# Recurrence gates of a hybrid encoder block: block pairs in the two row halves of the array, sigmoids by halves of the partitions, no Square

## The chip, the cores and the metric

The kernel runs on one core of a Trainium2 chip. TensorE (PE in the profile) does matmuls, VectorE (DVE) and ScalarE (ACT) work element by element, GpSimd (POOL) issues some transfers, and SyncE (SP) issues most of them. The metric is the device time of one execution in microseconds; less is better. Of several runs the median counts.

## The reference

One layer: half an FFN step, a mixing step with two branches, half an FFN step again, on x of 512 tokens by 1024 features, all in float32. The part that matters here is branch A, a recurrence that runs forward and backward over the tokens:

```python
def _rglru_scan(xc, w_gates, b_gates, lam):
    xb = xc.reshape(B_, S, LRU_BLOCKS, LRU_BLOCK)          # 16 blocks of 64 features
    gates = jnp.einsum('bsni,gnio->gbsno', xb, w_gates).reshape(2, B_, S, W)
    gates = gates + b_gates[:, None, None, :]
    r = sigmoid(gates[0]); i = sigmoid(gates[1])
    log_a = -LRU_C * r * softplus(-lam)                    # LRU_C = 8
    a = exp(log_a)
    bx = sqrt(-expm1(2.0 * log_a)) * (i * xc)
    h = scan of h[t] = a[t] * h[t-1] + bx[t]

xr, gr, q, k, v, ga, gb = split(rmsnorm(x) @ w_in)
xc = depthwise conv of width 4 over the tokens of xr
A = (h_forward + h_backward) * gelu(gr)
B = neighbourhood attention of q, k, v (q and k RMS-normed per head)
x = x + (sigmoid(ga) * A + sigmoid(gb) * B) @ w_out
```

Each of the 16 blocks has its own 64 by 64 weight for r and for i, and that for each of the two directions.

## The kernel before

Features lie on the partitions, 128 at a time, and tokens along the free dimension, 512 of them. A tile of 128 features thus holds two blocks of the recurrence. Float32 accuracy comes from splitting each operand in a high part H (float32r, made by ACT) and the rest L (made by DVE), and from three matmuls: `mm3` is H·H, H·L and L·H. `load_w` loads a weight by SP's queue and splits it; its splits have high priority, so they stand early in ACT's and DVE's order.

The mixing step first makes `xr` (eight tiles f, 24 matmuls each, in `acc` banks of PSUM), and `conv` after each. Then `tok_group` makes q, k and v for each half of the heads: 96 matmuls in four banks `acc`, with four weight loads. `qk_raw` has ACT empty the banks of q and k (copy, then Square and a sum on DVE for the norm); `v_get` has DVE empty those of v. PSUM has four banks `acc` and four `aux`.

The recurrence `lru` is a generator, run for f 0 to 3 and then for f 4 to 7 (here: the first half and the second half). `weave` calls it between the chunks of the other products, `RATE` steps at a time; `heads`, the attention, is a second such lane. For each f it makes gates for both directions d: the gate matmuls into `aux` banks, sigmoids on ACT, i times xc on DVE (tile `ix`), a tanh on ACT (tile `th`). When all eight (f, d) have that, it goes over them with exp, then roots, then the scans on DVE. With th = tanh(x), x = −log a, the kernel gets 1 − a² as (1 + a²)·th; Square makes a². So each activation table is loaded once in a half and not for every tile.

In `heads`, `rq` is one over the norm of q and k (`nc.scalar` Sqrt, then a reciprocal on DVE); eight multiplies scale the raw q and k tiles (`qk`); `start` transposes them and splits them into `qh`, `ql`, `kh`, `kl`; `scores` multiplies, with 64 rows a head, two heads side by side.

Instructions are written in this order, and the framework's scheduler sets the final order of each engine from priorities and its own estimates. `after(i, prev)` orders two instructions. An engine runs its own list in order; a wait on one holds all behind it.

Of the kernel before, what the change touches and what calls it, by code (L numbers as in the profile page):

```python
# [9 lines left out]
F32 = mybir.dt.float32  # L10
F32R = mybir.dt.float32r
AF = mybir.ActivationFunctionType
ALU = mybir.AluOpType
# [54 lines left out]
def block_kernel(ctx: ExitStack, tc, a, out):  # L68
# [27 lines left out]
    def aux_t():  # L96
        return aux.tile([P, T], F32, tag="aux", name=nm("aux"))
# [34 lines left out]
    def load_w(src, n, act=True):  # L132
        raw = raw_t()
        H, L = hl_t()
        s = slice(0, n)
        ld = nc.sync.dma_start(raw[:, s], src[:, s])
        if nld[0] < 8:
            tc.keep_in_program_order(ld)
        nld[0] += 1
        with tc.high_priority():  # L140
            split(raw[:, s], H[:, s], L[:, s], act)
        return H, L
# [53 lines left out]
        nc.scalar.activation(r, ps, AF.Copy)  # L196
        return r, rcol, vx

    def after(i, prev):

        i, prev = getattr(i, "ins", i), getattr(prev, "ins", prev)
        tc.add_manual_dep(i, prev.name, mybir.DependencyInfo(
            mybir.DependencyClass.NoSync, mybir.DependencyReason.DATA), reason="order")


    mark = {}
# [338 lines left out]
    sp = const.tile([P, 16], F32, name="sp")  # L545
    nc.vector.tensor_scalar(sp, nlam, 0.0, None, ALU.max)
    nc.vector.scalar_tensor_tensor(sp, pol, 2.0, sp, ALU.mult, ALU.add)
    sp8 = const.tile([P, 16], F32, name="sp8")
    nc.vector.tensor_scalar(sp8, sp, 8.0, None, ALU.mult)
    sn8 = const.tile([P, 16], F32, name="sn8")  # L550
    nc.vector.tensor_scalar(sn8, sp, -8.0, None, ALU.mult)
    gq8 = const.tile([P, 1], F32, name="gq8")
# [27 lines left out]


    last_act = [None]

    def lru(fs):
        un = []
        cuts = {}

        def cut(f):
            if f in fs:
                cuts[f] = big_t(F32R, n="ch"), big_t(F32R, n="cl")  # L590
                split(xc[f], *cuts[f])

        cut(fs[0])
        for f in fs:
            gH, gL = load_w(a["wgate"][f], T)
            cut(f + 1)
            cH, cL = cuts.pop(f)
            yield
            for d in range(2):
                rt = []  # L600
                for g in range(2):
                    q = d * 2 + g
                    s = slice(q * P, (q + 1) * P)
                    ps = aux_t()
                    mm3(ps, gH[:, s], gL[:, s], cH, cL, True, True)
                    t = big_t(n="gate")
                    i = nc.scalar.activation(t, ps, AF.Sigmoid, bias=small[:, C_BG + f * 4 + q : C_BG + f * 4 + q + 1])
                    if last_act[0] is not None:
                        after(i, last_act[0])
                    rt.append(t)  # L610
                r, ix = rt
                nc.vector.tensor_tensor(ix, ix, xc[f], ALU.mult)
                th = big_t(n="th")
                tanh = nc.scalar.activation(th, r, AF.Tanh, scale=sp8[:, f * 2 + d : f * 2 + d + 1])
                un.append((f, d, r, ix, th))
                yield
        for f, d, r, ix, th in un:
            exp = nc.scalar.activation(r, r, AF.Exp, scale=sn8[:, f * 2 + d : f * 2 + d + 1])
            after(exp, tanh)
            sq = big_t(n="a2")  # L620
            nc.scalar.activation(sq, r, AF.Square)
            nc.vector.scalar_tensor_tensor(th, sq, 1.0, th, ALU.add, ALU.mult)
            yield
        for f, d, av, ix, th in un:
            last_act[0] = nc.scalar.activation(th, th, AF.Sqrt)
            after(last_act[0], exp)
            nc.vector.tensor_tensor(ix, ix, th, ALU.mult)
            yield
        h = None
        for f, d, av, ix, th in un:  # L630
            if d == 0:
                h = th
                nc.vector.tensor_tensor_scan(h, av, ix, 0.0, ALU.mult, ALU.add)
            else:
                nc.vector.tensor_tensor_scan(th[:, ::-1], av[:, ::-1], ix[:, ::-1], 0.0, ALU.mult, ALU.add)
                nc.vector.tensor_tensor(h, h, th, ALU.add)
                A[f] = h
            yield
# [263 lines left out]
def layouts(inp):  # L902

    f = lambda n: np.asarray(inp[n])
    con = np.ascontiguousarray
    o = {}
    x = f("x")[0].reshape(ROWS, NCB, QC, KT, P)
    o["x"] = con(x.transpose(3, 4, 1, 0, 2)).reshape(KT, P, T)

    def feat(w):  # L910
        k, n = w.shape
        return con(w.reshape(k // P, P, n // P, P).transpose(2, 1, 0, 3)).reshape(n // P, P, k)

    for i in (1, 2):
        w = f(f"w_ffn{i}_gu")[0]
        g, u = feat(w[:, :DFF]), feat(w[:, DFF:])
        n = NPLAIN[i - 1]
        o[f"w{i}gu"] = con(np.stack([g, u], 1)[:n]).reshape(2 * n, P, D)

        b = np.stack([g, u], 0)[:, n:].reshape(2, (FT - n) // 2, 2, P, 2, D // 2)  # L920
        o[f"w{i}s"] = con(b.transpose(1, 4, 0, 3, 2, 5)).reshape((FT - n) // 2, 4, P, D)
        d = f(f"w_ffn{i}_down")[0].reshape(FT // 2, 2, P, 2, T)
        o[f"w{i}d"] = con(d.transpose(3, 0, 2, 1, 4)).reshape(2, FT // 2, P, 2 * T)
    w = f("w_in")[0].reshape(D, 7, D)
    o["wxr"] = feat(w[:, 0])
    o["wg3"] = np.concatenate([feat(w[:, c]) for c in (1, 5, 6)], 0)
    qkv = w[:, 2:5].reshape(4, 2, P, 3, 2, T)
    o["wqkv"] = con(qkv.transpose(3, 4, 0, 2, 1, 5)).reshape(6, 4, P, 2 * T)
    o["wout"] = feat(f("w_out")[0])
    wg = f("lru_w_gates")[0]  # L930
    bd = np.zeros((KT, P, 4, P), wg.dtype)
    for b in range(16):
        s = slice((b % 2) * 64, (b % 2) * 64 + 64)
        bd[b // 2, s, :, s] = wg[:, :, b].reshape(4, 64, 64).transpose(1, 0, 2)
    o["wgate"] = bd.reshape(KT, P, 4 * P)
    col = lambda v: np.asarray(v).reshape(-1, KT, P).transpose(2, 1, 0).reshape(P, -1)
    o["small"] = con(np.concatenate([
        col(f("norm_ffn1")[0]), col(f("norm_mix")[0]), col(f("norm_ffn2")[0]),
        col(f("conv_w")[0]), col(f("conv_b")[0]),
        col(f("lru_b_gates")[0].reshape(4, D)), col(f("lru_lambda")[0]),  # L940
        np.tile(f("q_norm")[0], 2)[:, None], np.tile(f("k_norm")[0], 2)[:, None]], 1))


    rp = f("rel_pos_bias")[0]
    t = np.full((NH, ROWS, QC, 3, 2, ROWS, QC), -1.0e30, rp.dtype)
    for ty, n in enumerate((0, 1, 3)):
        for p in range(QC):
            c = n * QC + QC - 1 - p
            cs = min(max(c - 8, 0), GW - 16)
            for k in range(cs, cs + 16):  # L950
                hf, kc = divmod(k - KSTART[n], QC)
                for r in range(ROWS):

                    t[:, r, p, ty, hf, :, kc] = rp[:, r : r + ROWS, k - c + 15]
    o["rpb"] = t.reshape(NH, P, 6 * P)
    return o
# [18 lines left out]
```

## Time and profile before

| | |
|---|---|
| three runs, median (lowest, highest) | 1137.01 us (1136.99, 1138.92) |
| the profiled execution | 1136.66 us |
| its span from first to last instruction | 1134.9 us |
| granted TensorE clock | 1.0 |
| PE, DVE, ACT busy | 1126.8, 837.1, 617.3 us |
| first gate matmul, and first of the second half | 384.21, 453.10 us |
| first scores | 524.87 us |

The profile's rows give start and duration in us, engine, line of the code, operation, what is written and read, shape, and a count where equal neighbours are merged; in brackets how long the engine was idle before, and on what. Matmuls overlap: each shows about 0.39 us for 512 columns though they start much closer together, so the distance of starts is what counts.

### The profile page before, as it was taken

The numbers are of one execution on the slowest core, as the hardware profiler recorded it, in microseconds if no ns is written. First come the engines' busy times: TensorE is split into PE (matmuls) and PEld (weight loads), VectorE is DVE, ScalarE is ACT, GpSimd is POOL, SyncE is SP. The second block draws the span as 40 slices with busy tenths as digits, with TensorE's granted clock in tenths as the row PEclk, the third lists the DMA queues.
The fourth block names the chain that finished last, engine by engine and source line by source line (L and its number), as shares of the span: only waits on it lengthen the run. The fifth ranks groups of instructions, "written<-read, shape, count | busy, mean of one in ns | idle before, by whom it ended". The sixth has DMA issues, their size and how long they took to land.

```text
span 1134.9 us, 17275 instructions
## 1 busy us (share of the span) xinstructions
PE 1126.8 (99%) x6874; PEld 994.4 (88%) x6874; DVE 837.1 (74%) x1288; ACT 617.3 (54%) x924; POOL 19.3 (2%) x52
## 2 busy tenths in 40 slices
PE   9999999999999999999999999999999999999998
PEld 7899999988888888888788887778999999998886
DVE  7898888884836779788855577758688888894542
ACT  8554544563624696995564266756445545464330
POOL 0000000000000000010110000000000000000000
PEclk9999999999999999999999999999999999999999
DMA  8242333443333352353443232345123333253421
GB/s 274 81 131 80 122 97 109 132 133 103 121 102 104 98 169 68 124 165 93 137 143 103 93 102 90 107 167 186 56 80 124 95 108 116 89 171 94 130 75 38
DMA packets 43554, 130.70 MB, mean 115 GB/s; under 512 B 5968, under 2 KB 8272, under 8 KB 43472
## 3 DMA queue, kind: packets, MB, share of 16 engines
q1 hardware_dynamic: 39600, 119.36, 33.6%
q0 software_dynamic: 3296, 9.97, 2.9%
q8 instruction: 54, 0.88, 0.3%
q10 hardware_dynamic: 576, 0.26, 0.1%
q14 instruction: 28, 0.23, 0.1%
HBM read 121.17 MB, written 8.39 MB: 114 GB/s over the span
## 4 chain that ended last, share of the span: by engine, by line
PE 95%; DVE 3%; ACT 2%; issue 0%; DMA 0%; DVEq 0%; ACTq 0%
PE acc L260 29%; PE acc L146 11%; PE acc L145 11%; PE acc L147 10%; PE aux L260 5%; PE aux L145 4%; PE aux L146 4%; PE aux L147 4%; PE acc L668 3%; PE acc L667 3%; PE acc L669 3%; PE aux L796 1%; DVE wl L121 1%; PE aux L785 1%; DVE so L769 1%; ACT wh L118 1%
## 5 line engine op out<-in xcount | busy, mean ns | idle before, releaser
L118 ACT ACTIVATE wh<-wraw 128x1024 fp32r<-128x1024 f32 (+3 forms) x242 | 241.4, 1000 | 323.5 <-PE acc L260 98.5
L121 DVE TENSOR_TENSOR wl<-wraw,wh 128x1024 fp32r<-128x1024 f32 (+3 forms) x254 | 291.5, 1151 | 131.0 <-ACT wh L118 130.4
L260 PE MATMUL acc<-s,wh 128*128 128x256 f32 x1216 | 220.6, 283 | 0.0
L260 PEld LDWEIGHTS acc<-s,wh 128*128 128x128 f32 x1216 | 188.8, 190 | 0.0
L260 PE MATMUL acc<-s,wl 128*128 128x256 f32 x608 | 172.1, 283 | 0.0
L145 PE MATMUL acc<-xh,wh 128*128 128x512 f32 x304 | 120.4, 396 | 0.0
L146 PE MATMUL acc<-xl,wh 128*128 128x512 f32 x304 | 119.5, 393 | 0.0
L147 PE MATMUL acc<-xh,wl 128*128 128x512 f32 x304 | 118.9, 391 | 0.0
L260 PEld LDWEIGHTS acc<-s,wl 128*128 128x128 f32 x608 | 115.8, 190 | 0.0
L260 PE MATMUL acc<-xh,wl 128*128 128x256 f32 x304 | 86.1, 283 | 0.0
L260 PE MATMUL acc<-xl,wh 128*128 128x256 f32 x304 | 86.1, 283 | 0.0
L260 PE MATMUL acc<-xh,wh 128*128 128x256 f32 x304 | 86.0, 283 | 0.0
L667 PE MATMUL acc<-wh,xh 128*128 128x512 f32 x192 | 75.5, 393 | 0.0
L668 PE MATMUL acc<-wh,xl 128*128 128x512 f32 x192 | 74.8, 390 | 0.0
L669 PE MATMUL acc<-wl,xh 128*128 128x512 f32 x192 | 74.8, 389 | 0.0
L294 DVE TENSOR_TENSOR wraw<-wraw,pair 128x1024 f32<-128x1024 f32 x57 | 69.6, 1221 | 0.8
L145 PE MATMUL aux<-hh,wh 128*128 128x512 f32 x176 | 68.5, 389 | 0.0
L146 PE MATMUL aux<-hl,wh 128*128 128x512 f32 x176 | 68.5, 389 | 0.0
L147 PE MATMUL aux<-hh,wl 128*128 128x512 f32 x176 | 68.5, 389 | 0.0
L146 PE MATMUL acc<-hl,wh 128*128 128x512 f32 x176 | 68.5, 389 | 0.0
L145 PE MATMUL acc<-hh,wh 128*128 128x512 f32 x176 | 68.5, 389 | 0.0
L147 PE MATMUL acc<-hh,wl 128*128 128x512 f32 x176 | 68.5, 389 | 0.0
(195 smaller groups left out, 2221.5 us busy)
## 6 DMA issues: line engine op xcount, KB each, us to landing
wraw<-wqkv SPq DMA_DIRECT2D x24, 512.0 KB, 3.6
wraw<-wg SPq DMA_DIRECT2D x24, 512.0 KB, 3.5
wraw<-w1d SPq DMA_DIRECT2D x22, 512.0 KB, 3.6
wraw<-w2d SPq DMA_DIRECT2D x22, 512.0 KB, 3.6
pair<-w2s SPq DMA_DIRECT2D x20, 512.0 KB, 3.6
wraw<-w2s SPq DMA_DIRECT2D x20, 512.0 KB, 3.6
wraw<-w1s SPq DMA_DIRECT2D x18, 512.0 KB, 3.6
pair<-w1s SPq DMA_DIRECT2D x18, 512.0 KB, 3.6
```

The source lines that it names most:

```text
L118: nc.scalar.activation(H, raw, AF.Copy)
L121: nc.vector.tensor_tensor(L, raw, H.bitcast(F32), ALU.subtract)
L145: nc.tensor.matmul(ps, wh, xh, start=first, stop=False)
L146: nc.tensor.matmul(ps, wh, xl, start=False, stop=False)
L147: nc.tensor.matmul(ps, wl, xh, start=False, stop=last)
L260: nc.tensor.matmul(o, w_[:, c], x_, start=first and m + k == 0 and w_ is H and x_ is xh_, stop=m + k == 4 and w_ is L, skip_group_check=True)
L294: nc.vector.tensor_tensor(t, t, o, ALU.add)
L667: nc.tensor.matmul(pss[j], xh[kk][:, tj], H[:, s], start=kk == 0, stop=False)
L668: nc.tensor.matmul(pss[j], xl[kk][:, tj], H[:, s], start=False, stop=False)
L669: nc.tensor.matmul(pss[j], xh[kk][:, tj], L[:, s], start=False, stop=kk == KT - 1)
L769: nc.vector.tensor_tensor_reduce(so[:, cs], ps[hp][:, cs], bm[:, BTYPE[n]], -1.0, 3.0e38, ALU.add, ALU.min, nmx[:, i : i + 1])
L785: nc.tensor.transpose(pT[:, q * P : (q + 1) * P], pt[:, q * P : (q + 1) * P], ident)
```

## The change

The gate weights were laid out as 128 by 128 matrices with two 64 by 64 blocks on the diagonal and zeros beside them: for each f and d one such matrix for r and one for i. Now they are packed without the zeros: rows 0 to 63 hold the weights of the tile's first block, rows 64 to 127 those of its second, and the 128 columns are r and i side by side. For each f and d there are two banks `ps[b]`, one a block; three matmuls of 64 rows fill each, and those of the two blocks alternate, so that they stand in the two row halves of the array. A bank then has r in its partitions 0 to 63 and i in 64 to 127, so four sigmoids of 64 partitions put the parts in place where two of 128 did. The load of `wgate` is half as wide.

The first matmul of a group waits for the last sigmoid of the group two before it (`evicted`). The Square goes: with th = tanh(x/2) the root of th times (1 + a) is the root of 1 − a², so DVE multiplies `ix` by (1 + a) where it multiplied `th` by (1 + a²).

```diff
-                rt = []
-                for g in range(2):
-                    q = d * 2 + g
-                    s = slice(q * P, (q + 1) * P)
-                    ps = aux_t()
-                    mm3(ps, gH[:, s], gL[:, s], cH, cL, True, True)
-                    t = big_t(n="gate")
-                    i = nc.scalar.activation(t, ps, AF.Sigmoid, bias=small[:, C_BG + f * 4 + q : C_BG + f * 4 + q + 1])
-                    if last_act[0] is not None:
-                        after(i, last_act[0])
-                    rt.append(t)
-                r, ix = rt
+                c = slice(d * P, (d + 1) * P)
+                ps = [aux_t() for _ in range(2)]
+                mm = None
+                for W, X in ((gH, cH), (gH, cL), (gL, cH)):
+                    for b in (0, 1):
+                        o = slice(b * HD, (b + 1) * HD)
+                        prev, mm = mm, nc.tensor.matmul(
+                            ps[b], W[o, c], X[o], start=W is gH and X is cH, stop=W is gL)
+                        if prev is not None:
+                            after(mm, prev)
+                        elif len(evicted) > 1:
+                            after(mm, evicted[-2], True)
+                r, ix = (big_t(n="gate") for _ in range(2))
+                q = C_BG + f * 4 + d * 2
+                for b in range(2):
+                    for g, t in enumerate((r, ix)):
+                        o = slice(g * HD, (g + 1) * HD)
+                        i = nc.scalar.activation(t[b * HD : (b + 1) * HD], ps[b][o], AF.Sigmoid,
+                                                 bias=small[o, q + b : q + b + 1])
+                        if last_act[0] is not None:
+                            after(i, last_act[0])
+                evicted.append(i)
                 nc.vector.tensor_tensor(ix, ix, xc[f], ALU.mult)
                 th = big_t(n="th")
-                tanh = nc.scalar.activation(th, r, AF.Tanh, scale=sp8[:, f * 2 + d : f * 2 + d + 1])
+                tanh = nc.scalar.activation(th, r, AF.Tanh, scale=sp4[:, f * 2 + d : f * 2 + d + 1])
...
             exp = nc.scalar.activation(r, r, AF.Exp, scale=sn8[:, f * 2 + d : f * 2 + d + 1])
             after(exp, tanh)
-            sq = big_t(n="a2")
-            nc.scalar.activation(sq, r, AF.Square)
-            nc.vector.scalar_tensor_tensor(th, sq, 1.0, th, ALU.add, ALU.mult)
+            nc.vector.scalar_tensor_tensor(ix, r, 1.0, ix, ALU.add, ALU.mult)
...
-            gH, gL = load_w(a["wgate"][f], T)
+            gH, gL = load_w(a["wgate"][f], 2 * P)
```

The scheduler also moves other work. Three places follow; names are tiles with their numbers, and a word in brackets is the engine that is waited for.

PE, the last f of the second half. Before, four gates of three matmuls in a row:

```order
L145 MATMUL aux_4757<-ch_4657,wh_4722 128x512 [waits Activation_49]
L146 MATMUL aux_4757<-cl_4658,wh_4722 128x512 [waits DVE_49]
L147 MATMUL aux_4757<-ch_4657,wl_4723 128x512
L145 MATMUL aux_4763<-ch_4657,wh_4722 128x512 [waits Activation_49]
L146 MATMUL aux_4763<-cl_4658,wh_4722 128x512
L147 MATMUL aux_4763<-ch_4657,wl_4723 128x512
L145 MATMUL aux_4772<-ch_4657,wh_4722 128x512 [waits Activation_49]
L146 MATMUL aux_4772<-cl_4658,wh_4722 128x512
```

Now two groups of three pairs, here with one matmul of the value product between them:

```order
L609 MATMUL aux_4769<-ch_4665,wh_4734 128x512 [waits PE_49,Activation_49]
L609 MATMUL aux_4770<-ch_4665,wh_4734 128x512 [waits PE_49]
L609 MATMUL aux_4769<-cl_4666,wh_4734 128x512 [waits DVE_49]
L609 MATMUL aux_4770<-cl_4666,wh_4734 128x512
L609 MATMUL aux_4769<-ch_4665,wl_4735 128x512
L609 MATMUL aux_4770<-ch_4665,wl_4735 128x512
L679 MATMUL acc_4591<-wh_4806,xh_3102 128x512
L609 MATMUL aux_4786<-ch_4665,wh_4734 128x512 [waits PE_49,Activation_49]
L609 MATMUL aux_4787<-ch_4665,wh_4734 128x512 [waits PE_49]
```

As many matmuls as before, and each group's first one waits for ACT.

ACT, start of the second half. Before:

```order
L607 ACT_TABLE_LOAD
L607 ACTIVATE gate_4551<-aux_4547,small 128x512
L118 ACTIVATE wh_4662<-wraw_4661 128x1024
L607 ACTIVATE gate_4557<-aux_4553,small 128x512
L614 ACTIVATE th_4560<-gate_4551,sp_3675 128x512
L607 ACTIVATE gate_4566<-aux_4562,small 128x512
L607 ACTIVATE gate_4572<-aux_4568,small 128x512
L614 ACTIVATE th_4575<-gate_4566,sp_3675 128x512
L118 ACTIVATE ch_4583<-xc_4084 128x512
L718 ACT_TABLE_LOAD
L718 ACTIVATE rq_4932<-rq_4932 128x64
```

Now:

```order
L620 ACT_TABLE_LOAD
L620 ACTIVATE gate_4555<-aux_4547,small 64x512
L118 ACTIVATE wh_4670<-wraw_4669 128x1024
L620 ACTIVATE gate_4556<-aux_4547,small 64x512
L620 ACTIVATE gate_4555<-aux_4548,small 64x512
L620 ACTIVATE gate_4556<-aux_4548,small 64x512
L627 ACTIVATE th_4562<-gate_4555,sp_3675 128x512
L620 ACTIVATE gate_4572<-aux_4564,small 64x512
L620 ACTIVATE gate_4573<-aux_4564,small 64x512
L620 ACTIVATE gate_4572<-aux_4565,small 64x512
L118 ACTIVATE wh_4734<-wraw_4733 128x256
L620 ACTIVATE gate_4573<-aux_4565,small 64x512
```

The eight sigmoids stand where four stood, and the root for `rq` (L718) with its table load is no longer between the f's: it stands behind the last exp of the half.

DVE, the scale of the raw q and k tiles. Before, it stood among the gates of the second half (L612 is i times xc):

```order
L719 RECIPROCAL rq_4932<-rq_4932 128x64
L121 TENSOR_TENSOR wl_4723<-wraw_4721,wh_4722 128x512
L724 TENSOR_TENSOR qk_4351<-qk_4351,rq_4932 128x512
L724 TENSOR_TENSOR qk_4356<-qk_4356,rq_4932 128x512
L724 TENSOR_TENSOR qk_4361<-qk_4361,rq_4932 128x512
L724 TENSOR_TENSOR qk_4366<-qk_4366,rq_4932 128x512
L121 TENSOR_TENSOR wl_4729<-wraw_4727,wh_4728 128x1024
L612 TENSOR_TENSOR gate_4631<-gate_4631,xc_3989 128x512
```

Now it comes behind all of them and behind the multiplies by 1 + a (L634), mixed with those by the root (L639), ahead of the scans:

```order
L634 SCALAR_TENSOR_TENSOR gate_4778<-gate_4777,gate_4778 128x512
L634 SCALAR_TENSOR_TENSOR gate_4795<-gate_4794,gate_4795 128x512
L731 RECIPROCAL rq_4932<-rq_4932 128x64
L639 TENSOR_TENSOR gate_4556<-gate_4556,th_4562 128x512
L639 TENSOR_TENSOR gate_4573<-gate_4573,th_4579 128x512
L736 TENSOR_TENSOR qk_4351<-qk_4351,rq_4932 128x512
L736 TENSOR_TENSOR qk_4356<-qk_4356,rq_4932 128x512
L736 TENSOR_TENSOR qk_4361<-qk_4361,rq_4932 128x512
L121 TENSOR_TENSOR wl_5079<-wraw_5077,wh_5078 128x1024
L736 TENSOR_TENSOR qk_4366<-qk_4366,rq_4932 128x512
L639 TENSOR_TENSOR gate_4634<-gate_4634,th_4640 128x512
```

The reciprocal and the eight multiplies moved from the middle of the gates to the queue that ends in `kl`.

More of the change, by code (lines that the diff above doesn't have):

```diff
@@ L197, in rstd, with after @@
         return r, rcol, vx
-    def after(i, prev):
+    def after(i, prev, sync=False):
         i, prev = getattr(i, "ins", i), getattr(prev, "ins", prev)
         tc.add_manual_dep(i, prev.name, mybir.DependencyInfo(
-            mybir.DependencyClass.NoSync, mybir.DependencyReason.DATA), reason="order")
+            mybir.DependencyClass.Sync if sync else mybir.DependencyClass.NoSync, mybir.DependencyReason.DATA), reason="order")
     mark = {}
@@ L547, in block_kernel @@
     nc.vector.scalar_tensor_tensor(sp, pol, 2.0, sp, ALU.mult, ALU.add)
-    sp8 = const.tile([P, 16], F32, name="sp8")
-    nc.vector.tensor_scalar(sp8, sp, 8.0, None, ALU.mult)
+    sp4 = const.tile([P, 16], F32, name="sp4")
+    nc.vector.tensor_scalar(sp4, sp, 4.0, None, ALU.mult)
     sn8 = const.tile([P, 16], F32, name="sn8")
@@ L582, in block_kernel @@
     last_act = [None]
+    evicted = []
     def lru(fs):
@@ L930, in layouts @@
     wg = f("lru_w_gates")[0]
[L931 to L935, printed above, removed]
+    o["wgate"] = con(wg.reshape(2, 2, KT, 2, 64, 64).transpose(2, 3, 4, 0, 1, 5)).reshape(KT, P, 4 * 64)
     col = lambda v: np.asarray(v).reshape(-1, KT, P).transpose(2, 1, 0).reshape(P, -1)
+    bg = f("lru_b_gates")[0].reshape(2, 2, KT, 2, 64).transpose(1, 4, 2, 0, 3).reshape(P, 4 * KT)
     o["small"] = con(np.concatenate([
```

2 lines of the change are left out of this document (1 added, 1 removed).

## The prediction

> **What bounds the kernel now.** I read the page first, then the busy time by stretches, then the timelines of PE, ACT and DVE around the gates.
>
> ```profile
> PE 1126.8 (99%) x6874; PEld 994.4 (88%) x6874; DVE 837.1 (74%) x1288; ACT 617.3 (54%) x924; POOL 19.3 (2%) x52
> PE 95%; DVE 3%; ACT 2%; issue 0%; DMA 0%; DVEq 0%; ACTq 0%
> ```
>
> PE carries the chain that ended last almost alone, so a matmul taken out can shorten the run. The averages of ACT and DVE (54% and 74%) say little about the gates, which all stand between 384 and 525 us. That part in five stretches (first half of the gates; the query product; the key product; second half of the gates with the value product; from there to the first scores):
>
> ```profile
> core 0: us, PE busy (x) PEld busy (x) DVE busy (x) ACT busy (x) POOL busy (x), PEclk, DMA share, GB/s
> 384.00:409.60 25.60, 25.60 (x113) 20.68 (x112) 21.38 (x29) 24.38 (x38) 2.54 (x8) 1.00 0.61 192
> 409.60:431.30 21.70, 21.70 (x97) 18.00 (x96) 17.30 (x24) 21.64 (x34) 0.00 (x0) 1.00 0.29 87
> 431.30:453.10 21.80, 21.80 (x97) 18.02 (x97) 21.19 (x32) 10.97 (x19) 0.00 (x0) 1.00 0.25 76
> 453.10:485.70 32.60, 32.60 (x145) 26.98 (x144) 23.82 (x34) 30.14 (x45) 1.35 (x3) 1.00 0.41 129
> 485.70:524.80 39.10, 39.10 (x177) 32.19 (x175) 34.18 (x46) 26.50 (x42) 2.92 (x5) 1.00 0.46 129
> ```
>
> Here ACT is nearly as full as PE: 24.38 of 25.60, 21.64 of 21.70, and 30.14 of 32.60. The change gives PE less to do and ACT more, in just these stretches.
>
> **PE's part.** The same timeline shows a plain run and the one place where matmuls of 64 rows already stand in pairs, the scores (L759):
>
> ```profile
> 453.10 0.39 PE L145 MATMUL aux<-ch,wh 128*128 128x512 f32 x1
> ...
> 524.55 0.39 PE L669 MATMUL acc<-wl,xh 128*128 128x512 f32 x1
> 524.87 0.38 PE L759 MATMUL aux<-kh,qh 64*128 64x256 f32 x2
> 525.09 0.28 PE L759 MATMUL aux<-kl,qh 64*128 64x256 f32 x2
> 525.21 0.28 PE L759 MATMUL aux<-kh,ql 64*128 64x256 f32 x2
> ...
> 525.56 0.28 PE L759 MATMUL aux<-kh,ql 64*128 64x256 f32 x2
> 525.78 0.66 PE L733 MATMUL aux<-ident,qk 128*128 128x128 f32 x4
> ...
> 526.63 0.48 PE L667 MATMUL acc<-wh,xh 128*128 128x512 f32 x1
> 526.94 0.39 PE L668 MATMUL acc<-wh,xl 128*128 128x512 f32 x1
> ```
>
> Matmuls of 512 columns follow each other every 0.227 us (the key product's 96 fill the 21.80 us of its stretch). A pair of 256-column ones in the two row halves takes 0.12 (525.09 to 525.21), about half of that, so a pair costs what its columns cost once; I take 0.227 for a pair of 512 columns. Gates now: 96 matmuls, 21.8 us. Afterwards: 48 pairs, 10.9. Saved: 10.9 us of PE.
>
> Every stretch of pairs also pays to get in and out. Entry: 0.32 where 0.227 is usual, +0.09. First pair: 0.22 for 0.12, +0.10. Exit: 525.56 to 525.78, again 0.22 for 0.12, +0.10. The first full matmul behind: 0.31 for 0.227, +0.08 (read behind transposes, its nearest row). Together 0.37 a stretch; as bounds, 0.20 (entry and one more) and 0.5. The order of the changed kernel has 12 stretches: 7 in the first half, where matmuls of other products stand between the groups, 5 in the second. That is 4.4 us, and PE alone keeps 6.5.
>
> **ACT's part.** Rows of the second half, and of groups:
>
> ```profile
> 454.89 1.28 ACT L607 ACT_TABLE_LOAD   x1
> 456.19 0.69 ACT L607 ACTIVATE gate<-aux,small 128x512 f32<-128x512 f32 x1
> 456.77 1.05 ACT L118 ACTIVATE wh<-wraw 128x1024 fp32r<-128x1024 f32 x1
> 457.72 0.68 ACT L607 ACTIVATE gate<-aux,small 128x512 f32<-128x512 f32 x1
> 458.29 0.72 ACT L614 ACTIVATE th<-gate,sp 128x512 f32<-128x512 f32 x1
> 458.90 1.26 ACT L607 ACTIVATE gate<-aux,small 128x512 f32<-128x512 f32 x2
> ...
> 462.60 0.26 ACT L718 ACTIVATE rq<-rq 128x64 f32<-128x64 f32 x1
> ...
> 487.16 3.77 ACT L618 ACTIVATE gate<-gate,sn 128x512 f32<-128x512 f32 x6
> ```
>
> ```profile
> L621 ACT ACTIVATE a<-gate 128x512 f32<-128x512 f32 x16 | 8.9, 617 | 0.0
> ```
>
> From start to start a sigmoid takes 0.57, a split of 1024 columns 0.95, a tanh 0.61, an exp 0.62. A Square, 0.62 long, counts as 0.52, since the next starts 0.1 before its end, and a `ch` split of the same size too. No ACT row covers 64 partitions. Bounds for the half sigmoid: 0.57 (a full one) and 0.285 (half of it). I take 0.57, because a split of 1024 columns is 1.05 long and a Square of 512 is 0.62 on the same 128 partitions: time goes with the columns, and these stay 512. So 64 half sigmoids replace 32 whole ones, +18.2 us of ACT; the 16 Squares (L621) go, −8.3; the gate weight splits halve in width, some −1.6 (an estimate, 0.2 each).
>
> The second half is then no longer PE's. From its first sigmoid to its last tanh ACT has 32 half sigmoids (18.2), 8 tanh (4.9), 7 splits of 1024 (6.7), two ch splits (1.0) and one half-wide gate weight split (0.3, an estimate): 31.1 us. PE has 96 full matmuls (21.8), 24 pairs (5.4) and 5 stretches' switches (1.9): 29.1. Before, PE needed 32.6 there, and ACT was busy for 30.14. The Trainium skill's page TensorEngine Tiling (Performance Considerations, PSUM Bottleneck) warns of this, that tiling speeds up the matmuls and not the emptying of PSUM; by that rule alone the second half would end 2.0 us after PE's sum, which is near what the steps below give from rows.
>
> **Second half, step by step.** T is the time from its first gate matmul, 453.10 before. ACT's table load is tied to the end of the key product, T 1.8 (454.89), and ends at 3.1. Each group's first matmul waits for the last sigmoid of the group two before it; a sigmoid's result is there some 0.15 after the next one starts (it is 0.69 long, the next starts at 0.57). The fourth group is free at T 8.1 but its sigmoid ends at 9.5: PE waits 1.5. The eighth is free at 24.4 and starts at 25.9: another 1.5. Then the value eviction: in DVE's order the four `v` stand behind the last group's multiply, which waits for ACT at T 32.7; first `v` out at 34.3, where PE wanted its bank at 32.4: 1.9. PE's total to the scores is 71.75 (524.87) − 5.4 + 1.9 + 4.9 = 73.1.
>
> DVE is later still. The reordered row scale of the attention (L719, L724 before; `rq`, `qk`) moves from 462.9 to behind the last exp:
>
> ```profile
> 462.89 0.55 DVE L719 RECIPROCAL rq<-rq 128x64 f32<-128x64 f32 x1 [0.88 <-ACT rq L718]
> ...
> 464.02 2.49 DVE L724 TENSOR_TENSOR qk<-qk,rq 128x512 f32<-128x512 f32 x4
> ...
> 517.57 1.20 DVE L633 TENSOR_TENSOR_SCAN th<-gate,gate 128x512 f32<-128x512 f32 x1
> 518.68 1.20 DVE L121 TENSOR_TENSOR wl<-wraw,wh 128x1024 fp32r<-128x1024 f32 x1
> 519.80 0.69 DVE L636 TENSOR_TENSOR th<-th,th 128x512 f32<-128x512 f32 x1
> ...
> 523.80 0.74 DVE L742 SCALAR_TENSOR_TENSOR kl<-aux,small,kh 128x512 fp32r<-128x512 f32 x1
> ```
>
> ACT: from 3.1, the 31.1 above, a table 1.3, 8 exp 5.0, one split 0.95 = T 41.4; table and `rq` root: 43.1. Then on DVE in one queue up to `kl`: reciprocal 0.5, 8 multiplies `qk` and 8 `gate` at 0.6 = 9.6, 4 reductions 2.4, 8 scans at 1.11 = 8.9, 4 adds 2.4, 5 splits at 1.13 = 5.7, small ones 0.4, `ql` and `kl` 1.4: 31.3. With 0.6 of waits on splits whose buffers PE frees late, `kl` is ready at T 75.0. Before, its matmul started at 525.09, T 72.0. Second half: 3.0 us worse.
>
> **First half.** The same count: 24 pairs save 5.4; 7 switches cost 2.6; the waits for sigmoids, with ACT now 4 us fuller (16 × 0.57 − 8 × 0.52 − 0.8), come to 1.3 in six places of 0.1 to 0.4, the last where the key product takes over banks that ACT empties. Net 1.5 us earlier at the second half's start. DVE, 21.19 of 21.80 busy in the stretch before, would let it come at most 2.6 earlier: the second half's first `cl` stands at the end of its queue.
>
> **The rest.** Halved loads of `wgate` (SP's queue) save bytes that nothing waits for. From the first scores on the engines' orders are the same, but for a handful of rows; what is late there stays late to the end. New scales and operands (`sp4`, `ix` for `th`) keep count and shape: 0, covered by equal rows.
>
> **Sum.** −1.5 + 3.0 = +1.5 us on the profiled 1136.66. The median of the runs, 1137.01, is 0.35 above that execution; on it I forecast 1138.5. A measurement tells about 0.2%, 2.3 us, from no change: this is inside.
>
> **Rivals.** (a) Slower: the first half gives nothing back. Place: ACT between 384 and 431, where it had 1.3 us free of 47.3 and gets 4 more; its query evictions free the key product's banks. Price: the 1.5 are lost, 1137.0 + 3.0 = 1140.0. It decides when the gain at the second half's start falls under 0.8. For it: those two stretches; against: by my count only 0.4 reaches PE there, and ACT is half empty next (10.97 of 21.80).
>
> (b) Faster: ACT keeps up, as it would if half the partitions took half the time (the lower bound 0.285: ACT's sum then is 22.0 against 29.1). PE's 6.5 stand whole: 1130.5. Against it: columns, not partitions, set the rows above. The Trainium skill's page ScalarE: Activation LUTs (Step-by-step: what each stage is for) says one element per cycle and lane whatever the function; by it 64 partitions take as long as 128. No row here shows it.
>
> (c) The pairs don't run side by side at 512 columns. Then first half +3.9, second 73.1 + 5.4 − 71.75 = 6.8: 1147.7. L759 speaks against it.
>
> **Numbers.** Forecast, within 0.2%: 0.50. (a) with all that ends over 1139.3: 0.33; (b) with all under 1134.7: 0.15; (c) 0.02. So faster 0.15, same 0.50, slower 0.35. The likeliest case alone spans 1136.8 (a switch at 0.20 in the first half's seven places, −1.2, and a DVE queue free of waits, −0.5) to 1140.9 (a switch at 0.5, +0.9, and (a)'s 1.5). The range reaches to 1134.0 for part of (b) and to 1141.5.
>
> **What would show it.** Pairs of `ch` 0.23 apart, 64x512 sigmoids near 0.68 long; PE idle before the fourth and eighth group of the second half and before the first product after it, 1.5 to 2 each; scores waiting for DVE `kl`; the second half's first gate matmul near 451.6 and the first `kl` matmul near 526.6 (453.10 and 525.09 before). I am wrong if ACT is not in one piece from T 3 to 41, or half sigmoids are shorter, or `kl` comes before PE.

## The result, and the profile after

The changed kernel takes 1149.63 us (median of four runs; 1148.88 to 1152.53) where the kernel before takes 1137.0: ratio 1.0114, 95% interval 1.0102 to 1.0126, 12.6 us slower. The forecast was 1138.5, with a range up to 1141.5; the direction that it thought second likeliest came, and by more than its range allowed. The profiled execution of the changed kernel took 1149.65 us, its span is 1147.9 (before 1134.9).

The profile page's busy times, and the shares of the chain that ended last:

```profile
PE 1127.2 (98%) x6874; PEld 986.5 (86%) x6874; DVE 834.8 (73%) x1288; ACT 631.1 (55%) x938; POOL 19.2 (2%) x52
...
PE 86%; ACT 9%; DVE 3%; issue 1%; DMA 0%; ACTq 0%; DVEq 0%
```

PE lost 9 points of the chain and ACT took 7 of them. The five stretches, cut at the same places of the program as before (window, its length, then busy time and count of PE, PEld, DVE, ACT and POOL, PE's granted clock, DMA share, GB/s):

```profile
384.00:410.60 26.60, 23.63 (x113) 16.18 (x113) 17.27 (x23) 26.05 (x37) 2.55 (x8) 1.00 0.55 177
410.60:436.00 25.40, 24.64 (x113) 19.48 (x110) 16.89 (x24) 24.99 (x35) 0.00 (x0) 1.00 0.24 74
436.00:457.40 21.40, 19.38 (x86) 15.48 (x86) 21.40 (x29) 14.78 (x27) 0.00 (x0) 1.00 0.20 56
457.40:496.20 38.80, 34.01 (x144) 24.62 (x142) 20.08 (x33) 36.91 (x53) 0.00 (x0) 0.87 0.39 112
496.20:537.70 41.50, 39.61 (x179) 32.47 (x178) 40.40 (x57) 27.61 (x39) 4.27 (x7) 1.00 0.45 121
```

Before, PE was busy all through these 141 us. Now it stands idle 5.75 us in the first three stretches (26.60 − 23.63, 25.40 − 24.64, 21.40 − 19.38), 4.8 in the fourth and 1.9 in the fifth, and in the fourth its granted clock is 0.87. ACT is the full engine: 26.05 of 26.60, 24.99 of 25.40, 36.91 of 38.80. What PE waited for, in the same part (total, times, longest):

```profile
PE aux L609 <- ACT gate L620: 8.4, 7, 2.4
PE acc L679 <- ACT qk L692: 2.0, 1, 2.0
PE aux L771 <- DVE kl L754: 1.9, 1, 1.9
PE acc L679 <- DVE v L703: 0.3, 1, 0.3
```

Two rows by tile give the place in time (durations smallest/median/largest in ns, then first and last start in us, here from the second half on): the gate matmuls of the second half and the scores' `kl`.

```profile
L609 PE MATMUL aux<-ch,wh x16: 392/493/792, 457.2 to 487.0; 64*128 64x512 f32 x16
L771 PE MATMUL aux<-kl,qh x12: 277/280/383, 538.0 to 558.8; 64*128 64x256 f32 x12
```

The second half starts at 457.2 (before 453.1; forecast 451.6) and the scores at 538.0 (before 525.1; forecast 526.6). That is 12.9 of the 13.0 us: all is lost ahead of the first scores, 4.1 in the first half and 8.8 in the second.

Where ACT's time goes is seen in three rows of its timeline and two by line. A row "x4" is four instructions back to back:

```profile
472.80 0.73 ACT L627 ACTIVATE th<-gate,sp 128x512 f32<-128x512 f32 x1
473.53 2.80 ACT L620 ACTIVATE gate<-aux,small 64x512 f32<-64x512 f32 x4
476.36 1.06 ACT L118 ACTIVATE wh<-wraw 128x1024 fp32r<-128x1024 f32 x1
```

```profile
L620 ACT ACTIVATE gate<-aux,small x64: 681/684/687, 386.1 to 494.4; 64x512 f32<-64x512 f32 x64
```

```profile
L607 ACT ACTIVATE gate<-aux,small x32: 666/684/712, 386.0 to 481.9; 128x512 f32<-128x512 f32 x32
```

A half sigmoid lasts as long as a whole one, 684 ns, as forecast. But four of them and the start of the next instruction fill 2.83 us (473.53 to 476.36): 0.70 each, a little over their length. Whole ones start 0.57 apart, because each starts 0.12 before its predecessor ends. In a row of halves that overlap is gone.

### The profile page after: what moved, and what is told of

Same layout as the page of the kernel before. It is cut to its first block, busy times and chain, and to the rows that moved or that the text cites. A ratio compares the mean times of both kernels' runs of the same rounds, so it can differ in the third digit from the quotient of the medians.

```text
span 1147.9 us, 17313 instructions
## 1 busy us (share of the span) xinstructions
PE 1127.2 (98%) x6874; PEld 986.5 (86%) x6874; DVE 834.8 (73%) x1288; ACT 631.1 (55%) x938; POOL 19.2 (2%) x52
## 4 chain that ended last, share of the span: by engine, by line
PE 86%; ACT 9%; DVE 3%; issue 1%; DMA 0%; ACTq 0%; DVEq 0%
PE acc L260 29%; PE acc L146 10%; PE acc L145 10%; PE acc L147 10%; PE aux L260 5%; ACT gate L620 4%; PE aux L145 3%; PE aux L146 3%; PE aux L147 3%; PE acc L679 2%; PE acc L680 2%; PE acc L681 2%; ACT wh L118 2%; PE aux L808 1%; DVE wl L121 1%
```

## The experiments

**The pitch by itself.** Chains of 12 sigmoids of 512 columns stood behind the last store of the kernel before. The patterns, with L for partitions 0 to 63, U for 64 to 127, W for all, input to output:

```
cw W-W   cll L-L   cuu U-U   clu L-U   csame as cboth, one PSUM bank
cin  L-L,U-L      cout L-L,L-U     cboth L-L,U-U    cswap L-U,U-L
cafter L-L,U-L,L-U,U-U     cgray L-L,L-U,U-U,U-L    cmix W-W,L-L
csbw W-W, read from SBUF   csb  L-L,U-U, read from SBUF
```

> The kernel before, with 14 chains of 12 sigmoids of 512 elements appended behind its last store; only the pitch (start to start) inside each chain is read. The trace of the changed kernel shows 0.697 us from one half sigmoid to the next where whole ones stood 0.569 apart. Theory 1, a change of the first input partition from one instruction to the next costs the overlap: whole chains (cw, csbw) 0.57; constant ranges (cll, cuu, clu) 0.57; cout (input constant, output alternates) 0.57; cin, cboth, cswap, cafter 0.70; cgray alternates 0.57 and 0.70. Theory 2, a change of the output's first partition costs it: cout, cboth, cswap 0.70, cin 0.57. Theory 3, an instruction on 64 partitions never overlaps with the one before it, whatever its range: cll, cuu, clu and all others 0.70, only cw and csbw 0.57, and cmix 0.57 into a whole and 0.70 into a half. Theory 4, the same PSUM bank read twice running costs it: only csame and cafter show 0.70.

Rows of its timeline (start, time from the first start to the last end, 12 instructions each):

```profile
1134.78 7.05 ACT L932 ACTIVATE cw<-acc,small 128x512 f32<-128x512 f32 x12
1141.64 7.01 ACT L932 ACTIVATE cll<-acc,small 64x512 f32<-64x512 f32 x12
...
1155.68 6.99 ACT L932 ACTIVATE clu<-acc,small 64x512 f32<-64x512 f32 x12
1162.68 8.45 ACT L932 ACTIVATE cin<-acc,small 64x512 f32<-64x512 f32 x12
1171.15 8.40 ACT L932 ACTIVATE cout<-acc,small 64x512 f32<-64x512 f32 x12
1179.56 8.40 ACT L932 ACTIVATE cboth<-acc,small 64x512 f32<-64x512 f32 x12
...
1221.61 6.99 ACT L932 ACTIVATE cmix<-acc,small 128x512 f32<-128x512 f32 x12
```

Chains with one range throughout take 7.0 us, 0.57 each (1134.78 to 1141.64 is 6.86 for 12), whether on 128 or 64 partitions and even when input and output lie in different halves (`clu`). Chains in which the first partition of the input or of the output changes take 8.4, 0.70 each (1171.15 to 1179.56 is 8.41 for 12). None of the four theories was right alone: theory 1 asked for 0.57 in `cout`, theory 2 for 0.57 in `cin`; either change costs the overlap, 0.13 us. The bias is read from the same partitions as the input, so the run can't tell a change of the input's first partition from one of the bias's. When SBUF is read the loss is much the same: 7.47 us for `csbw`, 8.92 for `csb`. Theories 3 and 4 fall (`cll`, `cmix`; `cin`). In the change all four halves of a group have a different pair of ranges, so any order of them pays.

The Trainium skill's page ScalarE: Activation LUTs (What ACT_TABLE_LOAD costs) says that activations back to back overlap by about 93 ns. The whole sigmoids come near it, with 0.115 (0.684 long, 0.569 apart); the halves show that here it holds only while the ranges stay.

**Two whole sigmoids.**

```
-  four activations of 64x512, r and ix put in place
+  for b, t in enumerate((r, ix)):
+      nc.scalar.activation(t, ps[b], AF.Sigmoid, bias=small[:, q + b : q + b + 1])
```

> The changed kernel, with the four half sigmoids of a group replaced by two whole ones of 128x512 on the two accumulators as they stand (r and i of the two blocks are then mixed in the tiles, so it computes something else; pairs, the wait on the evicted accumulator and the missing square stay). Theory A (the half sigmoids lengthen ScalarE's chain, which ends in the scores' first kl): first second-half gate matmul at about 452, first kl matmul about 70 us behind it or less (8 groups x (4 x 0.70 - 2 x 0.57) = 13 us less of ScalarE than in the changed kernel), no PE at half clock, time 1128 to 1133. Rival C (switching the array between whole and half rows is what costs): sigmoids do not matter, time stays at 1147 to 1150. Rival D (the reordered tail, row scaling behind the last exp, is what costs): kl about 79 behind the first gate matmul, time 1142 to 1148.

1131.64 us, ratio 0.995 (0.9935 to 0.9965). First gate matmul of the second half 451.6, first `kl` matmul 519.9, 68.3 behind it:

```profile
L609 PE MATMUL aux<-ch,wh x16: 392/444/493, 451.6 to 474.2; 64*128 64x512 f32 x16
L768 PE MATMUL aux<-kl,qh x20: 275/278/283, 519.9 to 559.5; 64*128 64x256 f32 x20
```

The rows of waits hold one of 0.9 on a sigmoid. Theory A held and C fell: pairs, the added wait and the missing square together are a gain of 5 us, and the 18 us between this and the changed kernel came with the half sigmoids. D isn't tested here: the `rq` root is back at its early place in this run (460.8; 506.3 in the changed kernel), so the 18 us include what its late place may cost.

**Four whole sigmoids**: as many as in the change, with one range.

```
+  for b in range(2):
+      for t in (r, ix):
+          nc.scalar.activation(t, ps[b], AF.Sigmoid, bias=small[:, q + b : q + b + 1])
```

> The changed kernel with each half sigmoid of a group replaced by a whole one of 128x512 on the same accumulator (each tile is then written twice over, so it computes something else): as many sigmoids as the changed kernel, in its order, but with one range of partitions throughout, which the chains of the last run show 0.573 apart in place of 0.70. Theory A1 (the lost overlap is most of the loss): 64 x 0.125 = 8 us less of ScalarE in all, the last exp about 42 us behind the second half's first gate matmul, the first kl matmul about 75 behind it, time 1138 to 1141, which was the forecast's own sum. Theory A2 (the number of sigmoids is what costs, their pitch hardly): 1146 to 1150.

1140.06 us (1138.39 to 1140.44), ratio 1.002 (1.001 to 1.0029). Its rows:

```profile
L609 PE MATMUL aux<-ch,wh x16: 390/493/501, 452.3 to 478.3; 64*128 64x512 f32 x16
L769 PE MATMUL aux<-kl,qh x16: 276/278/383, 527.1 to 557.0; 64*128 64x256 f32 x16
```

```profile
493.13 0.71 ACT L630 ACTIVATE gate<-gate,sn 128x512 f32<-128x512 f32 x1
...
495.14 0.26 ACT L728 ACTIVATE rq<-rq 128x64 f32<-128x64 f32 x1
```

Last exp out 41.5 us behind the first gate matmul, the `rq` root 43.1, `kl` 74.8. The forecast had 41.4, 43.1 and 75.0. Its waits are there too: 1.2 and 1.25 on sigmoids and 1.8 on `v`, for a forecast of 1.5, 1.5 and 1.9. A1 held: this is the kernel that the forecast had worked out. D falls here, since the root is late and `kl` is not at 79. So 32 sigmoids more at 0.57 cost 8.4 us (1131.64 to 1140.06), and the lost overlap 9.6 more (to 1149.63). The first of the two differences also holds the place of the `rq` root, early in the kernel with two sigmoids and late here; the run with the root early, below, bears on that but doesn't settle it.

**The halves without the pairs.**

```
-  t = sigmoid(ps)              # 128x512
+  for b in range(2):
+      o = slice(b * HD, (b + 1) * HD)
+      t[o] = sigmoid(ps[o])
```

> The kernel before, each of its 32 whole sigmoids cut into two of 64x512 (partitions 0 to 63, 64 to 127, in place); block-diagonal matmuls, square and order otherwise as before. Theory A: the cut alone adds 16 x (1.40 - 0.57) = 13 us to ScalarE's second half, PE's own work there is longer than in the changed kernel by 5 us and covers part of it: time 1143 to 1150, with waits of the gate matmuls on the sigmoids as in the changed kernel. Rival C (the array's switching costs, not the sigmoids): 1137 to 1139.

1161.52 us, ratio 1.0214 (1.0195 to 1.0232). Far outside the expectation, on the slow side: ACT keeps its squares and PE its full matmuls. First gate matmul 462.2, `kl` 547.7. PE waits 4.7 for the query evictions on ACT, 4.7 for `v`, 3.1 for `kl`, 3.1 for gates. C fell again. The size I had wrong mainly because I counted the second half alone, and 9 us were lost by its start.

**The square alone.**

```
-  sq = Square(r);  th = (sq + 1) * th
+  ix = (r + 1) * ix            # tanh of half the argument
```

> The kernel before with the square alone removed (tanh of half the argument; the exponential itself, not its square, enters the product, which goes into the input gate's tile). Theory A: 8 squares of 0.57 us = 4.6 us of ScalarE less in the second half: time 1132 to 1137. Rival D (the row scaling and the root move behind the last exponential with the square gone, as in the changed kernel, and that costs): 1139 to 1145.

1136.9 us, ratio 0.9991 (0.9981 to 1.0): no change to be told. Both marks stand where they stood, 453.1 and 525.0. ACT lost 8 us of work (609.3 busy for 617.3) and nothing waited for it: PE was full. The expectation's lower end was wrong for that reason. The order of D didn't come about: the root stayed at 462.6.

**The root early.**

```
+  with tc.high_priority():
       ... eight tensor_scalar, nc.scalar.activation(rq, rq, AF.Sqrt), reciprocal
```

> The changed kernel with one thing more: the first half of heads' norm (eight small tensor_scalar, the root of rq and its reciprocal) is given high priority, so that the root stands on ScalarE behind the second half's first sigmoid, as early as in the kernel before, and not behind the last exponential; it brings one more pair of activation tables (1.28 us each). Theory A3 (the late root makes the first kl wait for the whole ScalarE chain): kl about 75 us or less behind the first gate matmul, time 1142 to 1146, the rest of the loss being the gate matmuls' own waits. Theory A4 (the gate matmuls' waits on the sigmoids alone set the end, the root's place is nothing): 1148 to 1152, kl at 80 to 84.

1152.56 us, ratio 1.0129 (1.0114 to 1.0144): no faster than the change. A4 held, half a microsecond past its upper end.

```profile
463.70 1.28 ACT L731 ACT_TABLE_LOAD   x1
465.00 0.26 ACT L731 ACTIVATE rq<-rq 128x64 f32<-128x64 f32 x1
465.27 1.28 ACT L620 ACT_TABLE_LOAD   x1
```

```profile
PE aux L609 <- ACT gate L620: 8.7, 11, 1.2
PE aux L748 <- ACT gate L620: 2.5, 1, 2.5
PE acc L679 <- ACT qk L692: 2.1, 1, 2.1
```

The wait for `kl` is gone, as A3 says, but the root's two tables stretch the sigmoids' stretch, and PE waits there instead (`kl` 82.2 behind the first gate matmul). So moving the root up gains nothing while ACT is full. The place without the two table loads was not run.

**Other work off ACT**, the half sigmoids untouched: the high halves of some weight tiles are copied on VectorE.

```
-  load_w(a["wqkv"][w * 2 + hf, kp], 1024)
+  load_w(a["wqkv"][w * 2 + hf, kp], 1024, (w, hf) not in ((0, 0), (2, 0), (0, 1)))
-  feat_chunk(a["wxr"][f], KT, xh, xl, ps, 0, KT)
+  feat_chunk(a["wxr"][f], KT, xh, xl, ps, 0, KT, f < 4)
```

> The changed kernel, half sigmoids as they are, with ScalarE relieved of other work around the gates: the high halves of 12 of the weight tiles between gates (first q, first v, second q) and of the last four xr tiles are copied on VectorE (0.69 us each in the trace) and not on ScalarE (1.04). Theory A (ScalarE's total in this stretch is the bound, whatever the work is): 8 x 0.97 = 8 us less of it in the second half, so kl about 73 to 75 us behind the first gate matmul, and the second half begins 2 to 4 us earlier: 1138 to 1142. Rival C (only the sigmoids' own waits on accumulators count, so relief elsewhere does nothing): 1147 to 1150.

1141.27 us, ratio 1.0036 (1.0022 to 1.0051): 8.4 us back from the change, as A expects. `kl` stands 73.5 behind the first gate matmul (456.2 and 529.7). That start is 1.0 us earlier than in the change, where A had 2 to 4. Two more things differ from the change: the scheduler put the root early again (468.3), and PE's clock is 1.00 throughout. An early root alone had gained nothing in the last run, so the gain goes with ACT's total in this stretch; how much the full clock gave is not separated.

**The clock behind waits.** In the fourth stretch of the changed kernel PE was also slow. Its timeline behind one wait, the value in brackets being PE's idle time:

```profile
467.80 0.50 PE L609 MATMUL aux<-ch,wh 64*128 64x512 f32 x2 [2.37 <-ACT gate L620]
468.13 0.40 PE L609 MATMUL aux<-cl,wh 64*128 64x512 f32 x2
468.36 0.40 PE L609 MATMUL aux<-ch,wl 64*128 64x512 f32 x2
468.69 0.50 PE L679 MATMUL acc<-wh,xh 128*128 128x512 f32 x1
469.03 0.50 PE L680 MATMUL acc<-wh,xl 128*128 128x512 f32 x1
...
469.75 0.63 PE L679 MATMUL acc<-wh,xh 128*128 128x512 f32 x1
470.18 0.63 PE L680 MATMUL acc<-wh,xl 128*128 128x512 f32 x1
...
472.90 0.40 PE L681 MATMUL acc<-wl,xh 128*128 128x512 f32 x1
```

From 469.75 matmuls stand 0.43 apart where 0.227 is usual. To see what does that, trains of matmuls were put behind waits of chosen length.

```
for n in (1, 2, 3, 4, 5, 6, 8):      # n ScalarE copies between two trains
    hold(ps, n); ps = train(40)
for n in (2, 1):                     # then short trains behind waits
    for k in range(8): hold(ps, n); ps = train(6)
    hold(ps, 1); ps = train(40)
```

> The kernel before with trains of matmuls of 128x512 appended behind its last store: 60 at once, then 40 behind a wait of one ScalarE copy, of two, of three and so on to eight (some 0.9 to 6 us), then eight short trains of six matmuls each behind a wait of two copies, a train of 40, the same behind a wait of one, a train of 40. Theory K1 (the clock falls after one long wait): the trains behind the waits over about 2.3 us start at a pitch of 0.43 us and come back to 0.227 within some 5 us; those behind shorter waits run at 0.227 from the start, and the short trains too. Theory K2 (it falls with the share of idle time over some 10 us, however it is cut): the trains behind single waits stay at 0.227, and the short trains and what follows them run at 0.43.

```profile
1144.83 9.36 PE L911 MATMUL acc<-hold,idr 128*128 128x512 f32 x40 [0.69 <-ACT hold L920]
1155.54 9.36 PE L911 MATMUL acc<-hold,idr 128*128 128x512 f32 x40 [1.35 <-ACT hold L923]
1166.91 11.00 PE L911 MATMUL acc<-hold,idr 128*128 128x512 f32 x40 [2.01 <-ACT hold L923]
...
1225.89 11.17 PE L911 MATMUL acc<-hold,idr 128*128 128x512 f32 x40 [5.31 <-ACT hold L923]
...
1238.41 1.65 PE L911 MATMUL acc<-rep,idr 128*128 128x512 f32 x6 [1.35 <-ACT rep L923]
...
1261.75 9.36 PE L911 MATMUL acc<-hold,idr 128*128 128x512 f32 x40 [0.69 <-ACT hold L920]
```

K1 held with a lower bound than I had named: up to 1.35 us of idle time nothing happens, also when such waits take nearly half of the time eight times over; from 2.01 on each train costs 1.3 to 1.8 us more (10.69 to 11.17 for 9.36; 1.64 is 8 matmuls at 0.43), whatever the wait. Each of these longer waits was tried once, and in the kernels length alone does not decide. The run with weight copies on VectorE has a longer wait than the one above, and behind it matmuls stand 0.23 apart:

```profile
476.26 0.50 PE L609 MATMUL aux<-ch,wh 64*128 64x512 f32 x2 [2.60 <-ACT gate L620]
477.72 0.39 PE L681 MATMUL acc<-wl,xh 128*128 128x512 f32 x1
477.95 0.40 PE L679 MATMUL acc<-wh,xh 128*128 128x512 f32 x1
```

Two nearly equal waits for the query evictions show it too: behind 2.02 us (until 439.30) the changed kernel keeps its full clock, and behind 2.06 us (until 439.25) the run with the root early falls to 0.54 from 441.0 to 444.5. Behind the changed kernel's other long wait on a sigmoid (2.42 us, until 487.01) the slow stretch was twice as long: from 486.4 to 493.2 the granted clock is 0.51. The Trainium skill's page TensorE: Matmul & The Clock Gate (What's actually happening) tells of a window of 3.41 us that runs freely and halves the clock when it was idle. The slow stretches of 3.4 us, and of 6.8, agree with it; that 2.01 us of idle time were enough is less than a whole window, and there the measurement counts.

**Directions in the halves of the partitions.** If half sigmoids are what costs, the pairs should be had without them. Here a pair computes one gate for both directions, so r and the input gate lie in the same place and nothing crosses partitions until the scan.

```
-  ps[b] = [r_b ; i_b]          # one direction, columns of wgate: gate, channel
+  ps[b] = [g_b forward ; g_b backward]   # one gate g of block b
+  for b in range(2): sigmoid(gt[b, g] <- ps[b])          # 128x512
+  nc.gpsimd.dma_start(xw[b] halves <- xc[f], block b)    # 4 for each tile
-  2 scans of 128x512 for a tile
+  4 scans of 64x512, b and direction, written to block b's partitions
```

> Another way to the same pairs, with the reference's result: each pair computes one gate for both directions (columns 0 to 63 forward, 64 to 127 backward) of its two blocks, so every tile holds one block with its directions in the two halves of the partitions, and r and the input gate lie in the same place. Sigmoids are whole again, two for a group; the convolved tile is copied to both halves by four DMAs on GpSimd's queue; what moves between halves is the scan's result, by 32 scans over 64 partitions in place of 16 over 128 (1.13 us apart each in the changed kernel: 18 us more of VectorE, 9 in each half). Theory A (ScalarE's sigmoids were the loss and VectorE has room): as the kernel with two whole sigmoids, 1130 to 1134, no PE at half clock, kl about 69 behind the first gate matmul. Rival (VectorE becomes the bound before the scores): kl 73 to 78 behind it, 1137 to 1142.

1149.34 us, ratio 1.0106 (1.0089 to 1.0123): as slow as the change, for another reason. The rival named the engine, but its price was far too low: `kl` is 84.7 behind the first gate matmul (450.9 and 535.6).

```profile
PE aux L776 <- DVE kl L759: 6.8, 1, 6.8
PE aux L611 <- DVE cl L121: 5.5, 1, 5.5
PE aux L611 <- ACT gate L620: 0.5, 1, 0.5
```

ACT is no longer waited for (0.5). VectorE is, at the end of each half's scans:

```profile
446.34 1.22 DVE L651 TENSOR_TENSOR_SCAN th<-gate,gate 64x512 f32<-64x512 f32 x1
447.57 1.22 DVE L650 TENSOR_TENSOR_SCAN th<-gate,gate 64x512 f32<-64x512 f32 x1
```

A scan over 64 partitions is 1.22 us long like one over 128, and in this alternation of ranges the next starts 1.23 behind it.

**The same with another order on VectorE.**

```
+  with tc.high_priority(): split(xc[f], ...), and the splits of q and k
+  after(scan, mark["kl"])      # the last tile's four scans
```

> The kernel of the last run with the directions in the two halves of the partitions, which lost two waits of TensorE on VectorE (5.5 us for cl before the second half's gates, behind the first half's scans; 6.8 us for kl before the first scores, behind the second half's): the splits of the convolved tile and of q and k get high priority, and the last tile's four scans stand behind the first kl. Theory A (with VectorE's queue in another order the pairs bring what they bring with two whole sigmoids): 1132 to 1138, no wait above 2 us before the scores. Rival (VectorE's 18 us more come back elsewhere, in the attention): 1141 to 1148.

1145.04 us, ratio 1.0071 (1.0056 to 1.0086). A fell. The time is in the rival's range, but not the place: the two waits went (`kl` 1.2), and one of 6.1 us came up ahead of the scores, at the next place where a split stands behind the first half's scans. In neither order did VectorE have room for 18 us in front of the scores.

**DMAs in place of the additional scans.**

```
-  4 scans of 64x512
+  8 DMAs of 64x512: scan input, then decay, of both blocks to one tile for each direction
+  2 scans of 128x512
```

> The kernel with the directions in the two halves of the partitions and two whole sigmoids for a group, but with 16 scans over 128 partitions as before: ahead of the scans eight DMAs of 64x512 for each tile put the decay and the scan's input of the two directions side by side (GpSimd's queue, 64 DMAs in all beside the 32 for the doubled convolved tile). Theory A (ScalarE's half sigmoids were the loss, and neither ScalarE nor VectorE has more work now than with two whole sigmoids): 1131 to 1135, kl 68 to 71 us behind the first gate matmul. Rival (the transfers come late and VectorE, which takes its queue in order, stands at the scans with the splits and kl behind it): 1138 to 1146.

1140.21 us (1137.33 to 1143.17), ratio 1.0027 (1.0014 to 1.004). The rival's time and its mechanism: PE waits 2.6 for a `cl` and 2.6 for a `ql` that stand behind scans. `kl` is early (522.1, which is 65.6 behind the first gate matmul; that one stands later in PE's order here, at 456.5).

> As the last, with the 64 DMAs for the scans on SyncE's queue, where the weight loads are: issue is shorter there, but a DMA that waits for the square roots' products holds the weight loads behind it. Theory A: 1131 to 1135 as well. Rival (weight loads come late): 1138 to 1150 with TensorE waiting on splits of wraw.

The same with these DMAs issued by SyncE: 1132.27 us (1131.14 to 1134.95), ratio 0.9954 (0.9939 to 0.997). This one computes the layer, which the kernel with two whole sigmoids doesn't. It beats both kernels and comes within 1 us of that one. A held and the rival fell. PE's waits up to the scores:

```profile
PE aux L611 <- ACT gate L620: 0.5, 1, 0.5
```

## Why the prediction was wrong

**The pairs: right.** They run side by side (468.13 to 468.36: 0.23), and the switch costs 0.10 at the first pair, 0.10 at the exit and 0.11 at the first full matmul in the rows above; the forecast's 0.37 for a stretch had 0.28 for these three. With the sigmoids out of the way the kernel takes 1131.6, 1.1 above rival (b)'s 1130.5, which had PE's 6.5 us whole.

**The price of a half sigmoid: the step that failed.** The forecast took 0.57 and called it the upper bound, from the row of a whole sigmoid. Its argument, that time goes with the columns and not with the partitions, is right for the length: 684 ns both. But 0.57 is no length. It is a length less the overlap with the neighbour, and the overlap depends on the neighbour. It measured 0.70. The row for a bound without overlap was in the forecast's own fence, a sigmoid 0.69 long at 456.19, with the next start at 456.77 beside it.

**What hung on it.** ACT from the second half's first sigmoid to its last tanh: forecast 31.1, measured 37.7 (460.00 to 497.70). The half sigmoids make 4.0 of the difference: 30 of the 32 hold ACT 0.13 longer, and two, each in front of a weight split, don't. The way into the halves from another instruction (a tanh takes 0.73 in front of a half sigmoid, 472.80 to 473.53, where it was 0.61) adds about 1.4 in 11 places, an estimate at 0.13 each; 1.0 is idle. Everything behind followed as forecast: the `rq` root behind the last exp, DVE's chain from the reciprocal to the end of `kl` 31.2 us (506.74 to 537.97; forecast 31.3), the scores waiting for DVE `kl` (1.9). So `kl` came at 80.8 and not at 75.0. The run with four whole sigmoids, whose pitch is the forecast's 0.57, gives back the forecast's own figures.

**The first half.** Forecast 1.5 earlier, measured 4.1 later: 5.75 us of idle time where 1.3 was counted. It is the same term: ACT was to be 4 us fuller there, and 32 half sigmoids at 0.13 more make it 8, an estimate, in stretches where the forecast itself found 1.3 us free of 47.3. The idle time is 4.5 of the 5.6 us between forecast and run; the rest was not taken apart. Rival (a) named the place, but took its price, 1140.0, from the same 0.57.

**Waits.** Gate matmuls waited for sigmoids, as said, but for 4.8 us in the second half, not 3.0, and for 3.6 in five places of the first. The value eviction's wait (forecast 1.9) was 0.3; the key product's wait for the query evictions on ACT, counted among small ones, was 2.0.

**Not in the forecast at all**: PE's slow stretches behind long waits. At 0.87 of the clock over 34.0 us of busy time they are some 4 us of PE in the second half, an estimate. Since PE still had to wait 1.9 for `kl` behind them, most of the second half's end is not theirs; no run took them away alone, so their share of the loss is open. Up to 1.0 us of the end may be theirs, since ACT's idle 1.0 us (until 496.02) is a wait for PE behind one of them.

**The square and the rest: right.** The square's removal by itself is worth nothing that can be told (0.9991), and no run shows a cost of the added wait on an evicted accumulator.

## What to carry to other kernels

Price an instruction in a queue by start to start, and ask of each new neighbour whether the overlap survives: on ScalarE here it did on 64 partitions as on 128, but not when the first partition of input or output changed (0.57 against 0.70). Halving TensorE's work by tiling its rows was paid here where the results are emptied; so lay the outputs out such that whole instructions can empty them, and leave what must cross partitions to DMAs off the path (1132 us in place of 1150). When an engine next in line has 1 us free of 47, an error of a fifth in its price can be the whole result, so the range should be made by that term's worst reading, its full length.

## What was not expected of the hardware

- In chains of sigmoids ScalarE loses 0.13 us of overlap at every change of the first partition of input (with its bias) or output, at unchanged length; not by 64 partitions as such, and reading one PSUM bank twice is not needed for it. Open is why a half sigmoid behind a tanh or a copy over all partitions is late too (0.736 for 0.614 behind a tanh): in the chains whole and lower-half sigmoids alternate at 0.57.
- A scan on VectorE over 64 partitions takes as long as over 128 (1.22 us), and in alternating halves it stands 1.23 to 1.25 apart where whole ones stand 1.13.
- About 2 us of idle TensorE can be enough for 3.4 us at half clock, or for 6.8; 1.35 us were not, in eight short waits on end. Length alone does not decide: waits of 2.01, 2.06, 2.37 and 2.42 us had the effect, and 2.02 in the changed kernel and 2.60 in the run with weight copies on VectorE had none. No run here shows what decides.
